# Turning six heads of a latent attention off TensorE, and dividing softmax rows on ScalarE

## The chip, the cores and the metric

The kernel runs on one core of a Trainium2 chip. The metric is device microseconds for one launch, lower is better. Before the change the median of three runs is 986.88 us (985.52 to 986.89). The profile shown here is of one execution that took 986.1 us, of which 984.3 us are the span from the first to the last recorded instruction.

## The reference: what is computed

A sequence of 256 tokens of width 1024 passes through two layers. Each layer is a half-step SwiGLU feed-forward block, a token mixer, a second half-step feed-forward block and a gated embedding; a last normalisation ends it. Layer 0 mixes with multi-head latent attention (chunk-causal, with a rotary part), layer 1 with forgetting attention (token-causal, with a decay bias). Both have 8 heads of width 128 and share this core:

```python
s = scores_fn(q0, q1)                        # (B, H, 128, q1), float32
s = jnp.where(allowed, s, NEG_INF)
probs = jax.nn.softmax(s, axis=-1).astype(v.dtype)
outs.append(jnp.einsum('bhqk,bkhd->bqhd', probs, v[:, :q1]))
```

The queries come in two blocks of 128; block 0 sees 128 keys, block 1 all 256. So one head has a score tile of 128 rows (queries) by 384 columns: 128 columns for block 0, then 256 for block 1.

## The kernel before, in words

Everything is float32. Weights come from memory as raw tiles of 128 x 1024; ScalarE rounds each to a high part (L97) and VectorE takes the rest as a low part (L101), so that the matrix products of high and low parts on TensorE keep float32 accuracy. `Weights` keeps four raw tiles and seven pairs; its transfers (L88) are issued on SyncE's queue, in the order in which the program calls it.

Every engine takes its own instructions strictly in program order. The order is written out by hand: there is no scheduler that moves an instruction past another. So an instruction that waits holds up whatever stands behind it on its engine or on its transfer queue.

`attention` (L487) is called by both mixers and is a software pipeline over steps h. In step h it does, in this order:

- `shares(h-2)`: VectorE takes the reciprocal of the softmax sums (L520) and multiplies the two parts of the row tile by it (L521, L522).
- `low()`: VectorE computes the low part of head outputs that are pending (L565, recorded at L228).
- `project(h, 0)`: the first half of what makes queries and keys of a later head. In the latent attention that is at most some products and their copies to SBUF (L707 to L721); in the forgetting attention it is a whole block of eight weight products.
- some "fills" (`fill_some`): products of finished heads with the output weights, put in to keep TensorE busy.
- the turn of a head, so that keys lie on the partitions, as the value product wants them.
- `scores(h-1)`: the score products on TensorE, then on VectorE the masked copy with its row maximum (L501) and the bias (L505 or L510/L511), then two exponentials with row sums on ScalarE (L513, L514).
- `project(h, 1)`, a weight tile's low part in some steps, more fills.
- `values`: the value products (L557, L558), and the copy of the result to SBUF by ScalarE (L559).

There are two ways to turn a head. `turn` (L539) uses TensorE: three 128 x 128 transposes (L543) into PSUM, then a copy to SBUF on ScalarE (L545). The other way is used for heads below `moved`: VectorE transposes the 32 x 32 blocks of the tile (L526), four transfers on SyncE's queue write it to memory so that whole rows come to lie right (L531), and `back` (L533) reads it in again with one transfer (L536).

The two mixers differ in their parameters. The latent attention (`mla`, L787) has `lag` 3, which the code calls `late`, and `moved` 0: every head is turned on TensorE in step h = head + 3 and its values follow in the same step. The forgetting attention (`fox`, L889) has `lag` 2 and `moved` 6: heads 0 to 5 go through memory and get their values one step after `back`, heads 6 and 7 are turned on TensorE. The fills per step are fixed tables: `MLA_FILLS` (L45) gives, for the latent attention, 3 fills in step 6, 4 in step 7, 1 + 5 in step 8, 4 + 3 in step 9 and 2 + 2 in step 10. `ready` (L620, L638) says for how many heads a fill may be made; a fill that is not possible yet is left for the loop behind the pipeline (L647). Four output blocks (`early`) are open for fills.

In the latent attention, step 1 also issues four transfers of rotary query parts on SyncE's queue (L720, L721), and step 3 four more.

## Time and profile before

| what | value |
|---|---|
| median of 3 runs | 986.88 us (985.52 to 986.89) |
| the profiled execution | 986.1 us, span 984.3 us |
| TensorE (PE) busy | 975.3 us |
| VectorE (DVE) busy | 735.5 us |
| ScalarE (ACT) busy | 507.4 us |
| GpSimd (POOL) busy | 428.2 us |
| steps of the latent attention | about 212 to 246 us of the span |
| steps of the forgetting attention | about 688 to 748 us of the span |

The profile has a page of totals and several views of the same trace. The timeline of an engine lists its instructions with start and duration in us; in brackets stands how long the engine had been idle before and who released it. Starts of neighbouring rows give the real pace, since instructions of one engine overlap at their ends. The view of one source line gives the shortest, middle and longest duration in ns of its instructions and, for a transfer, the time from its issue to its landing. PE is TensorE, SPq is the queue of transfers that SyncE issues.

### The profile page before, as it was taken

How to read it: one execution, taken by the hardware profiler on the slowest of the kernel's cores; microseconds unless marked ns; L12 is line 12 of the kernel's file. 1: busy time of each engine (PE TensorE's matmuls, PEld its weight loads, DVE VectorE, ACT ScalarE, POOL GpSimd, SP SyncE). 2: the span in 40 equal slices, each digit the busy share in tenths (PEclk: the TensorE clock that was granted, in tenths of full speed). 3: DMA queues.
4: the chain of work that ended last, by engine and by line, in shares of the span. 5: the costliest groups of instructions: out<-in, count | busy, mean ns of one | idle time of the engine just before them, and what ended most of it. 6: DMA issues, size and time to landing. Idle time of an engine off the chain costs nothing.

```text
span 984.3 us, 15934 instructions
## 1 busy us (share of the span) xinstructions
PE 975.3 (99%) x5766; PEld 861.4 (88%) x5766; DVE 735.5 (75%) x1097; ACT 507.4 (52%) x796; POOL 428.2 (44%) x374
## 2 busy tenths in 40 slices
PE   9999999999999999999999999999999999999997
PEld 7888888998988888889888888889889888888886
DVE  6777878686867787667887876666997677786585
ACT  7555544466545554545555544545445455544361
POOL 0777731110357775111477773122231377771010
PEclk9999999999999999999999999999999999999999
DMA  8677666564456666665367666557773566666581
GB/s 324 187 250 208 199 184 183 185 197 124 127 161 210 213 204 188 190 201 194 107 199 212 196 183 197 176 174 240 234 214 113 180 192 209 207 194 192 137 280 56
DMA packets 67166, 187.53 MB, mean 191 GB/s; under 512 B 18724, under 2 KB 21168, under 8 KB 66960
## 3 DMA queue, kind: packets, MB, share of 16 engines
q1 hardware_dynamic: 65904, 183.94, 61.2%
q0 software_dynamic: 608, 1.72, 0.5%
q8 instruction: 46, 0.75, 0.3%
q10 hardware_dynamic: 576, 0.85, 0.3%
q14 instruction: 32, 0.26, 0.1%
HBM read 181.88 MB, written 2.24 MB: 187 GB/s over the span
## 4 chain that ended last, share of the span: by engine, by line
PE 94%; DVE 2%; ACT 1%; issue 1%; DMA 1%; POOL 0%; SPq 0%; POOLq 0%; DVEq 0%; ACTq 0%
PE po L247 17%; PE pu L247 16%; PE pg L247 16%; PE po L248 8%; PE pg L248 8%; PE pu L248 8%; PE ps L247 5%; PE ps L248 2%; PE ps L234 2%; PE ps L232 2%; PE ps L233 2%; PE pv L232 1%; PE pv L234 1%; PE pv L233 1%; PE po L557 1%; DVE wlo L101 1%
## 5 line engine op out<-in xcount | busy, mean ns | idle before, releaser
L101 DVE TENSOR_TENSOR wlo<-raw,whi 128x1024 fp32r<-128x1024 f32 (+2 forms) x339 | 416.4, 1235 | 28.3 <-ACT whi L97 28.1
L97 ACT ACTIVATE whi<-raw 128x1024 fp32r<-128x1024 f32 (+2 forms) x339 | 336.0, 1023 | 40.6 <-DMA raw<-in_ffn_in_dram 14.7
L390 POOL TENSOR_TENSOR gu<-two 128x256 f32<-128x256 f32 x176 | 217.7, 1238 | 113.7 <-DVE two L388 107.1
L247 PE MATMUL pg<-u,whi 128*128 128x512 f32 x702 | 251.2, 395 | 0.0
L247 PE MATMUL pu<-u,whi 128*128 128x512 f32 x702 | 250.9, 395 | 0.0
L247 PE MATMUL po<-hs,whi 128*128 128x512 f32 x704 | 246.8, 394 | 0.0
L248 PE MATMUL pg<-u,wlo 128*128 128x256 f32 x702 | 197.3, 281 | 0.5 <-DVE wlo L228 0.3
L248 PE MATMUL po<-hs,wlo 128*128 128x256 f32 x704 | 197.3, 280 | 0.0
L248 PE MATMUL pu<-u,wlo 128*128 128x256 f32 x702 | 196.8, 280 | 0.0
L247 PEld LDWEIGHTS po<-hs,whi 128*128 128x128 f32 x704 | 132.1, 188 | 31.3
L247 PEld LDWEIGHTS pu<-u,whi 128*128 128x128 f32 x702 | 131.8, 188 | 31.0
L247 PEld LDWEIGHTS pg<-u,whi 128*128 128x128 f32 x702 | 131.8, 188 | 30.9 <-ACT whi L1099 0.2
L248 PEld LDWEIGHTS pg<-u,wlo 128*128 128x128 f32 x702 | 132.0, 188 | 2.0 <-DVE wlo L101 1.1
L248 PEld LDWEIGHTS po<-hs,wlo 128*128 128x128 f32 x704 | 132.3, 188 | 0.0
L248 PEld LDWEIGHTS pu<-u,wlo 128*128 128x128 f32 x702 | 132.0, 188 | 0.0
L408 POOL TENSOR_TENSOR hid<-sg,gu 128x256 f32<-128x256 f32 x88 | 121.1, 1376 | 6.9
L303 POOL TENSOR_TENSOR acc<-acc,sq 128x256 f32<-128x256 f32 x42 | 43.2, 1028 | 178.6 <-ACT sq L298 156.3
L224 ACT ACTIVATE hs<-hid 128x256 fp32r<-128x256 f32 x88 | 36.8, 418 | 155.7 <-POOL hid L408 155.7
L228 DVE TENSOR_TENSOR hs<-hid,hs 128x256 fp32r<-128x256 f32 x88 | 54.1, 615 | 71.3 <-ACT hs L224 71.3
L287 ACT ACTIVATE u<-state 128x256 fp32r<-128x256 f32 x47 | 24.0, 511 | 122.7 <-DVE state L467 102.4
L388 DVE TENSOR_TENSOR two<-pg,rb 128x512 f32<-128x512 f32 x88 | 60.0, 682 | 28.9 <-PE pg L248 19.4
L467 DVE SCALAR_TENSOR_TENSOR state<-po,state 128x256 f32<-128x256 f32 x64 | 27.1, 424 | 60.2 <-PE po L248 59.1
(258 smaller groups left out, 1157.6 us busy)
## 6 DMA issues: line engine op xcount, KB each, us to landing
raw<-in_ffn_in_dram SPq DMA_DIRECT2D x172, 512.0 KB, 4.2
raw<-in_ffn_out_dram SPq DMA_DIRECT2D x64, 512.0 KB, 4.2
raw<-in_ffn_out_dram SPq DMA_DIRECT2D x32, 384.0 KB, 3.4
raw<-in_fox_qk_dram SPq DMA_DIRECT2D x16, 512.0 KB, 4.4
raw<-in_mla_o_dram SPq DMA_DIRECT2D x8, 512.0 KB, 5.9
raw<-in_ple_gate_dram SPq DMA_DIRECT2D x8, 512.0 KB, 4.2
raw<-in_fox_o_dram SPq DMA_DIRECT2D x8, 512.0 KB, 3.9
raw<-in_ple_rows_dram SPq DMA_DIRECT2D x8, 512.0 KB, 4.8
```

The costliest lines, as they stand in the source:

```text
L97: self.nc.scalar.activation(self.pairs[i][0][:, c], self.raws[i][:, c], AF.Copy)
L101: self.nc.vector.tensor_sub(lo[:, c], self.raws[i][:, c], hi[:, c].bitcast(F32))
L224: nc.scalar.activation(hi, src, AF.Copy)
L228: nc.vector.tensor_sub(lo, src, hi.bitcast(F32))
L232: nc.tensor.matmul(ps, w[0], x[0], start=first, stop=False)
L233: nc.tensor.matmul(ps, w[1], x[0], start=False, stop=False)
L247: nc.tensor.matmul(ps, hi, x[:, k], start=k == 0, stop=False)
L248: nc.tensor.matmul(ps[:, 1, :], lo, x[:, k, 0, :], start=False, stop=k == last)
L303: nc.gpsimd.tensor_add(new, self.acc, sq)
L388: nc.vector.tensor_mul(two, ps, norm.rb2)
L390: nc.gpsimd.tensor_add(gu[c, i], two[:, 0, :], two[:, 1, :])
L408: nc.gpsimd.tensor_mul(hid[c], gu.pop((c, 0)), gu.pop((c, 1)))
```

## The change

In both attentions the two multiplications by the reciprocal go, for heads below `moved`, from VectorE to ScalarE (a copy with a scale for each partition). What followed them in `shares` becomes a function `out`, called after `low()`: the block transpose on VectorE, then one transfer that writes the tile as it lies. `back` now gathers: four transfers, each of 32 partitions with four pieces of 96 numbers. In the forgetting attention all four are on SyncE's queue; in the latent attention two of them are on GpSimd's queue.

The latent attention gets `moved` 6. Its heads 0 to 5 are no longer turned on TensorE; `back` for a head stands at the start of step head + 3, behind `out` of the next head, and its values stand at the end of step head + 4. Heads 6 and 7 are as they were. The first `ready` of a step is one lower while moved heads are under way. The blocks are kept in a part of the `kqv` tile that lies idle. `MLA_FILLS` does not change. Pending low parts are now done in the order in which they came.

```diff
--- before.py
+++ after.py
@@ -518,22 +518,28 @@
             pr, den = probs[h]
             inv = work.tile([P, 2], F32, name="inv", bufs=3)
             nc.vector.reciprocal(inv, den)
-            nc.vector.tensor_scalar(pr[:, :P], pr[:, :P], inv[:, 0:1], None, op0=ALU.mult)
-            nc.vector.tensor_scalar(pr[:, P:], pr[:, P:], inv[:, 1:2], None, op0=ALU.mult)
-            if h < moved:
-                pr, _ = probs.pop(h)
-                squares = room[h % 2]
-                nc.vector.transpose(squares.rearrange("p (k u c) -> p k u c", k=4, u=3),
-                                    pr.rearrange("p (u k c) -> p k u c", u=3, k=4))
-                turned[h] = dram.tile([P, 3 * P], F32, name="keys", bufs=2)
-                to = turned[h].rearrange("(k r) (q n) -> q r k n", k=4, q=4)
-                for q in range(4):
-                    nc.sync.dma_start(to[q], squares[q * 32:(q + 1) * 32, :].rearrange("r (k n) -> r k n", k=4))
+            for i, a in enumerate((slice(0, P), slice(P, 3 * P))):
+                if h < moved:
+                    nc.scalar.activation(pr[:, a], pr[:, a], AF.Copy, scale=inv[:, i:i + 1])
+                else:
+                    nc.vector.tensor_scalar(pr[:, a], pr[:, a], inv[:, i:i + 1], None, op0=ALU.mult)
+
+        def out(h):
+
+            pr, _ = probs.pop(h)
+            squares = room[h % 2]
+            nc.vector.transpose(squares.rearrange("p (k u c) -> p k u c", k=4, u=3),
+                                pr.rearrange("p (u k c) -> p k u c", u=3, k=4))
+            turned[h] = dram.tile([P, 3 * P], F32, name="keys", bufs=3)
+            nc.sync.dma_start(turned[h], squares)
 
         def back(h):
 
             p = work.tile([P, 3 * P], F32, name="ptS", bufs=3)
-            nc.sync.dma_start(p, turned[h])
+            src = turned[h].rearrange("(q r) (k n) -> k r q n", q=4, k=4)
+            for k in range(4):
+                (nc.gpsimd if late and k % 2 else nc.sync).dma_start(
+                    p[k * 32:(k + 1) * 32, :].rearrange("r (q n) -> r q n", q=4), src[k])
             turned[h] = p
 
@@ -562,7 +568,7 @@
             while lows:
-                rest(*lows.pop())
+                rest(*lows.pop(0))
@@ -613,15 +619,19 @@
             if 0 <= h - 2 < H:
                 shares(h - 2)
             low()
+            if 0 <= h - 2 < moved:
+                out(h - 2)
+            if late and 0 <= h - lag < moved:
+                back(h - lag)
             if h == H and not late:
                 W.pump()
             if late:
 
-                ready = h - lag - 1
+                ready = h - lag - 1 - (0 < h - lag <= moved)
             if h < H:
                 project(h, 0)
             fill_some(fills.get((h, 0), 0))
-            if 0 <= h - lag < moved:
+            if not late and 0 <= h - lag < moved:
                 back(h - lag)
             if moved <= h - lag:
                 turn(h - lag)
@@ -689,6 +699,7 @@
         kT, qT, qr = kq[:, :8, :], kq[:, 8:16, :], kq[:, 16:24, :]
+        squares = [kr[:, a:a + 2, :].rearrange("p s n -> p (s n)")[:, :3 * P] for a in (2, 4)]
@@ -784,7 +795,7 @@
-        attention(project, score, v, lambda h: (chunks[:, P:], chunks), qscale, nxt, 3, MLA_FILLS, 4)
+        attention(project, score, v, lambda h: (chunks[:, P:], chunks), qscale, nxt, 3, MLA_FILLS, 4, moved=H - 2, room=squares)
```

## The prediction

> **What bounds the kernel now.** I read the page first, then the waits, then the timelines of the engines in the latent attention, then the transfers.

> ```profile
> span 984.3 us, 15934 instructions
> PE 975.3 (99%) x5766; PEld 861.4 (88%) x5766; DVE 735.5 (75%) x1097; ACT 507.4 (52%) x796; POOL 428.2 (44%) x374
> ...
> PEclk9999999999999999999999999999999999999999
> ...
> PE 94%; DVE 2%; ACT 1%; issue 1%; DMA 1%; POOL 0%; SPq 0%; POOLq 0%; DVEq 0%; ACTq 0%
> ```

> ```profile
> PE cold L1090 <- DVE warm L1087: 1.1, 1, 1.1
> ```

> TensorE (PE) is busy 975.3 of 984.3 us, and 94% of the chain that ended last is its work. The longest wait of PE in the trace is 1.1 us, at the start. So any product removed is time gained, and any new wait of PE is time lost, wherever PE stands in its order. What has to be asked is whether the six heads' keys are in SBUF when PE comes to their values.

> The rows of PE in the latent attention, each with its start and duration:

> ```profile
> 218.81 0.49 PE L543 MATMUL pt<-ident,pr 128*128 128x128 f32 x3
> ...
> 222.24 0.49 PE L543 MATMUL pt<-ident,pr 128*128 128x128 f32 x3
> 222.57 0.82 PE L782 MATMUL psc<-kqv 128*128 128x128 f32 x4
> ...
> 224.58 0.61 PE L557 MATMUL po<-ptS,kqv 128*128 128x256 f32 x2
> ...
> 225.25 0.49 PE L543 MATMUL pt<-ident,pr 128*128 128x128 f32 x3
> ...
> 231.07 0.59 PE L557 MATMUL po<-ptS,kqv 128*128 128x256 f32 x2
> ...
> 232.05 0.82 PE L782 MATMUL psc<-kqv 128*128 128x128 f32 x4
> ...
> 234.77 0.60 PE L557 MATMUL po<-ptS,kqv 128*128 128x256 f32 x2
> ...
> 245.77 0.48 PE L247 MATMUL ps<-os,whi 128*128 128x512 f32 x1
> ...
> 246.54 0.39 PE L247 MATMUL ps<-os,whi 128*128 128x512 f32 x1
> ...
> 246.89 0.40 PE L247 MATMUL ps<-os,whi 128*128 128x512 f32 x1
> ```

> By starts: a turn costs PE 0.33 us (222.24 to 222.57), not the 0.49 of its row; scores with the six or three products behind them 2.01 (222.57 to 224.58); values 0.67 (to 225.25), 0.65 where fills follow; a fill 0.35 (246.54 to 246.89); scores with four fills 2.72 (232.05 to 234.77), so scores alone 1.32 and with three fills 2.37. The values of head 3 start at 231.07; those of head 7 are over at 245.77.

> VectorE and ScalarE hand each head to and fro, and that loop has a time of its own:

> ```profile
> 218.06 0.16 DVE L520 RECIPROCAL inv<-den 128x2 f32<-128x2 f32 x1
> ...
> 226.96 0.17 DVE L520 RECIPROCAL inv<-den 128x2 f32<-128x2 f32 x1 [0.64 <-ACT pr L514]
> ...
> 227.62 0.42 DVE L228 TENSOR_TENSOR os<-po,os 128x256 fp32r<-128x256 f32 x1
> 227.96 0.28 DVE L501 CUSTOM_DVE_ANT_0 pr<-psc,chunks 128x128 f32<-128x128 f32 x1
> ...
> 228.62 0.16 DVE L505 SCALAR_TENSOR_TENSOR nm<-m,qscale 128x2 f32<-128x2 f32 x1
> ...
> 230.08 0.17 DVE L520 RECIPROCAL inv<-den 128x2 f32<-128x2 f32 x1 [0.64 <-ACT pr L514]
> ```

> ```profile
> 228.88 0.49 ACT L513 ACTIVATE pr<-pr,nm,qscale 128x128 f32<-128x128 f32 x1 [1.31 <-DVE nm L505]
> 229.28 0.19 ACT L513 ACTIVATION_READ_ACCUMULATOR pr<-pr,nm,qscale 128x1 f32 x1
> 229.37 0.58 ACT L514 ACTIVATE pr<-pr,nm,qscale 128x256 f32<-128x256 f32 x1
> ```

> From reciprocal (226.96) to reciprocal (230.08) it is 3.12 us: 0.66 for reciprocal and divisions, 0.34 for the low part of an older head, 0.66 for the masked copies, then 0.26 to the first exponential, and 1.20 for both until the next reciprocal, for which VectorE has waited 0.64. PE's own step there is 3.01 (222.24 to 225.25). Both are close; a longer loop is not hidden for long.

> **The change, part by part.**

> *Turns removed.* Six of the eight turns of the latent attention go from PE: 6 x 0.33 = 1.98 us. This is all that PE can gain, and nothing else of PE's work changes but order. The strided read of the value product costs nothing extra: forgetting attention reads so already, at the same pace (row 708.38 below). The six copies out of PSUM on ScalarE go too; they were in nobody's way.

> *Divisions on ScalarE, and the transpose in the loop.* VectorE's next masked copy now stands behind the transpose, that behind ScalarE's two divisions, and those behind the reciprocal. The nearest row for a division is a copy with a scale per partition; for the transpose it is the forgetting attention's:

> ```profile
> L287 ACT ACTIVATE u<-state 128x256 fp32r<-128x256 f32 x47 | 24.0, 511 | 122.7 <-DVE state L467 102.4
> ```

> ```profile
> 698.25 0.16 DVE L520 RECIPROCAL inv<-den 128x2 f32<-128x2 f32 x1
> ...
> 699.03 0.58 DVE L526 STREAM_TRANSPOSE kqv<-pr 128x384 f32<-128x384 f32 x1
> 699.54 0.65 DVE L872 TENSOR_TENSOR two<-ps,rb 128x512 f32<-128x512 f32 x1
> ...
> 722.40 0.69 DVE L872 TENSOR_TENSOR two<-ps,rb 128x512 f32<-128x512 f32 x1 [0.20 <-PE ps L248]
> ```

> The division of 128 x 256 takes 0.51, that of 128 x 128 0.09 less (as the two exponentials differ), and the second starts 0.09 before the first ends (228.88 + 0.49 against 229.28): 0.84 for both. With 0.17 for the reciprocal and hand-overs of 0.10 and 0.04 (the bias ends at 228.78, its exponential starts at 228.88), the transpose starts 1.15 us after the reciprocal, and the masked copy 0.51 later. The older head's low part now falls into the wait for ScalarE. New loop: 1.15 + 0.51 + 2.12 (227.96 to 230.08) = 3.78 us against 3.12, in six steps. Bounds: 3.6 if ScalarE takes 0.66 like VectorE now, 3.9 if its pair does not overlap.

> So reciprocals, which start in step 2 at 218.06, come 3.78 apart, as 221.84, 225.62, 229.40, 233.18 and 236.96 for heads 1 to 5, and each transpose ends 1.73 after its own: heads 0 to 4 at 219.79, 223.57, 227.35, 231.13 and 234.91.

> *The way through memory.* The rows of the forgetting attention, of GpSimd's queue, and of SyncE's queue in the steps in question:

> ```profile
> L531 SPq DMA_DIRECT2D keys<-kqv x24: 318/426/678, 699.6 to 734.5; - x24
> ...
> DMA to landing us min/median/max: 2.0/2.7/3.4
> ```

> ```profile
> L536 SPq DMA_DIRECT2D ptS<-keys x6: 337/338/338, 703.5 to 736.7; - x6
> ...
> DMA to landing us min/median/max: 2.7/3.1/4.0
> ```

> ```profile
> L352 POOL DMA_DIRECT2D rb<-row x3: 577/577/582, 274.4 to 776.5; - x3
> ...
> DMA to landing us min/median/max: 3.3/4.4/5.0
> ```

> ```profile
> 220.03 1.32 SPq L88 DMA_DIRECT2D raw<-in_mla_o_dram  x2
> ...
> 703.49 0.34 SPq L536 DMA_DIRECT2D ptS<-keys  x1
> ```

> No row shows a write of a whole tile or a gather in four; I bound the write by 2.0 to 3.4 and take 2.7, a piece on SyncE's queue by 2.7 to 4.0 and take 2.9, one on GpSimd's by 3.3 to 5.0 and take 4.4, the medians of the nearest rows (the pieces are smaller than the reading row's). An issue costs 0.43 on SyncE, 0.58 on GpSimd, which does nothing else in these steps. `back` of a head stands behind `out` of the next one on SyncE's queue, so its pieces there wait for the next head's transpose: that is the wait the change adds, and behind it stand four rotary transfers and weight tiles, whose users come later.

> Now PE's order. Step 3 starts at 218.81. Without turn and values, two times 2.01 brings PE to the values of head 0 at 222.83. Their keys: the first of the two weight tiles goes out on SyncE at 220.03 and I put the write behind it, at 220.6; it lands at 223.3 or, as loads of 512 KB are under way, up to 225.0; the next head's write is issued at 223.6, and the pieces on SyncE follow from 224.1 to 224.5 and land at about 227.4; those on GpSimd land from 223.3 + 0.58 + 4.4 = 228.3 on. I take 228.3: **PE waits 5.5 us.** Then the later heads:

> - Head 1: PE comes at 228.3 + 0.65 + 2.01 = 230.96. Keys: transpose of head 2 ends at 227.35, + 0.05 + 0.40 + 0.43 + 2.9 = 231.1, GpSimd's 223.6 + 2.7 + 0.58 + 4.4 = 231.3. Values at 231.3.
> - Head 2: PE at 231.3 + 0.65 + 2.37 = 234.3; keys at 231.13 + 3.8 = 234.9. Values at 234.9.
> - Head 3: PE at 234.9 + 0.65 + 2.72 = 238.3; keys at 234.91 + 3.8 = 238.7, GpSimd's at 231.17 + 2.7 + 0.58 + 4.4 = 238.85. Values at 238.7.
> - Head 4 and on: PE has 0.65 + 0.35 + 1.32 + 5 x 0.35 = 4.07 us of work first and comes at 242.8, keys at 242.5: no more waits.

> From there to the end of head 7's values it took 245.77 - 231.07 = 14.70 before. Of that fall away two turns (0.66), the scores of head 6 (1.32) and four fills (1.40), which now lie ahead; one fill of step 9 finds `ready` too low and is made behind the pipeline instead, the same 0.35 of work. So the same work is done at 238.7 + 11.3 = 250.0 against 245.8: **+4.2 us**. That is 1.98 gained and about 6.2 more of waiting. Bounds: with 2.0 for writes and 2.7 for all pieces, head 0 at 227.1 and the chain by PE alone gives head 3 at 236.1, +1.7; with 3.4, 4.0 and 5.0 head 3 is at 240.2, +5.7. Behind this PE is the bound again and nothing is given back.

> [...]

> *The forgetting attention.* PE does the same. On VectorE, reciprocal to the next product goes from 1.29 (698.25 to 699.54, no older head pending) to 1.15 + 0.51 = 1.66; with a low part of 0.3 pending, which the new order hides, it is about even. VectorE waits 0.20 for PE in such steps (722.40), so two steps of + 0.37 are made up. ScalarE has room:

> ```profile
> 722.29 0.40 ACT L513 ACTIVATE pr<-pr,nm 128x128 f32<-128x128 f32 x1 [3.63 <-DVE nm L511]
> ```

> ```profile
> 708.38 0.59 PE L557 MATMUL po<-ptS,kqv 128*128 128x256 f32 x2
> ```

> Head 0's keys landed near 703.49 + 3.1 = 706.6 and were wanted at 708.38. Transpose 0.4 later, three issues fewer and three more of 0.43: about 0.4 later in all, covered by 1.8. I take 0, with - 0.2 and + 0.8 as ends (nothing that PE waits for goes away; VectorE's 0.74 wholly passed on).

> *The rest* (order of pending low parts, a third buffer for keys) costs nothing: PE has fills between.

> Sum: 986.1 + 4.2 = 990.3 against the profiled execution. The median of the runs is 0.8 above that execution; I put half of it on top: **990.7**.

> **The rivals.**

> *The waits stay hidden* (faster). Two steps between transpose and values cover the way through memory, and only the 1.98 of the turns is left: 986.1 - 2.0 + 0.4 = 984.5. It decides at 2.0 us of PE's waits in all. For it: a step more was given. Against it: 222.83 minus 219.79 leaves 3.0 us for a write and a read that take 2.7 and 3.1 one after the other.

> *One wait, then PE sets the pace.* The loop stays near 3.3, or the transfers land early; PE waits once for head 0 and then follows its own work: + 1.7 to + 2.9, say 989.2.

> *The clock falls.* PE has no wait of over 1.1 us now and its granted clock stands at nine tenths or more in all 40 slices. If 5.5 us of idleness halved its rate until it waits again, 2.66 us of work between heads 0 and 1 become 5.3, head 1 comes at 233.6, head 2 at 236.6, head 3 at 240.0: + 5.5, 992.0. [...] Slow transfers (+ 5.7) end in the same place.

> **How the numbers follow.** Forecast 0.50, one wait 0.20, clock or slow transfers 0.15, waits hidden 0.07, an end within 2 us of before 0.08. 0.2% (2.0 us) is about what a measurement can tell. Slower: the forecast, the clock and most of "one wait", 0.82; the same 0.11; faster 0.07. The range takes the forecast, one wait and the clock, and their bounds: 987.8 to 993.2.

> **What would show it right or wrong.** In the changed profile: no rows of L543 before step 9 of the latent attention; PE idle some 4 to 6 us ahead of the first L557 there, released by a transfer of `ptS`; shorter idles ahead of the next three; reciprocals 3.7 to 3.9 us apart in steps 2 to 7; a wait of VectorE for ScalarE of 0.3 to 0.8 us ahead of each transpose; PE in the forgetting attention without waits. It is wrong if the first L557 waits under 2 us, if reciprocals stay near 3.1 apart, or if PE waits in the forgetting attention.

## The result, and the profile after

| | median | lowest to highest | profiled execution | its span |
|---|---|---|---|---|
| before | 986.82 us | 985.52 to 990.31 | 986.1 us | 984.3 us |
| after | 996.42 us | 994.99 to 998.59 | 994.99 us | 993.2 us |

The ratio is 1.0099, with a 95% interval of 1.0086 to 1.0113: 9.6 us slower, where the forecast was 3.9 and the range ended at 993.2. The sign was right and the size too small.

The page of the changed kernel: span and busy time, the granted clock in 40 slices, the chain that ended last.

```profile
span 993.2 us, 15932 instructions
PE 976.2 (98%) x5748; PEld 860.9 (87%) x5748; DVE 731.8 (74%) x1079; ACT 514.1 (52%) x814; POOL 434.8 (44%) x386
...
PEclk9999999998999999999999999999999999999999
...
PE 86%; DVE 5%; DMA 3%; ACT 2%; issue 2%; SPq 1%; POOL 1%; POOLq 0%; ACTq 0%; DVEq 0%
```

PE has 18 products fewer and is yet busy 0.9 us longer: some of its work has become slower. One digit of the clock's row, the tenth, is an 8. That slice is 223 to 248 us, in the latent attention. The chain now runs for 3% over transfers (1% before).

The waits of PE, in all, times, longest:

```profile
PE po L563 <- DMA ptS<-keys: 5.5, 1, 5.5
PE po L563 <- issue: 1.5, 1, 1.5
...
PE pst L317 <- POOL acc L303: 1.0, 1, 1.0
PE ps L247 <- DVE os L228: 0.3, 1, 0.3
```

L563 is the value product, L557 before. The wait for GpSimd (L303) lies at 960.23, in the last norm: e1 below has it too (0.91), e9, the changed kernel again, has not. From PE's timeline the first rows of heads 0, 1 and 5, the scores behind heads 0 and 1, and the product that follows head 7's values:

```profile
228.19 1.19 PE L563 MATMUL po<-ptS,kqv 128*128 128x256 f32 x2 [5.54 <-DMA ptS<-keys]
229.60 1.49 PE L793 MATMUL psc<-kqv 128*128 128x128 f32 x4
...
233.00 0.59 PE L563 MATMUL po<-ptS,kqv 128*128 128x256 f32 x2
233.66 0.82 PE L793 MATMUL psc<-kqv 128*128 128x128 f32 x4
...
249.25 0.67 PE L563 MATMUL po<-ptS,kqv 128*128 128x256 f32 x2 [1.46 <-issue]
...
253.28 0.48 PE L247 MATMUL ps<-os,whi 128*128 128x512 f32 x1
```

PE waits 5.54 us for head 0 and 1.46 for head 5. Heads 1 to 4 wait for nothing. The values of head 7 are over at 253.28, where the forecast had 250.0. Right behind the first wait scores take 1.49 us, a head later 0.82. The table by stretches of 2 us gives the reason; its columns are busy time of PE, of the weight loads, of VectorE, ScalarE and GpSimd, then the granted clock, the share of the DMA engines and GB/s:

```profile
224.00:226.00 2.00, 0.00 (x0) 0.00 (x0) 0.64 (x3) 1.65 (x6) 0.95 (x2) 0.91 0.85 311
226.00:228.00 2.00, 0.00 (x0) 0.00 (x0) 1.85 (x7) 0.74 (x3) 0.88 (x3) 0.50 0.64 174
228.00:230.00 2.00, 1.81 (x6) 1.67 (x7) 0.17 (x1) 0.59 (x3) 0.42 (x1) 0.50 0.64 153
230.00:232.00 2.00, 2.00 (x9) 1.73 (x7) 1.00 (x2) 0.91 (x3) 0.90 (x2) 0.50 0.39 114
232.00:234.00 2.00, 2.00 (x11) 1.72 (x11) 1.52 (x6) 0.72 (x3) 0.18 (x1) 0.88 0.63 176
```

The clock falls to 0.50 inside the wait and comes back at about 232.5 (0.88 is 0.5 for the first 0.48 us). PE works from 228.19 to then at half rate: 4.3 us in which 2.1 us of work are lost.

**Where the time lies.** I measure one stage: from the last norm ahead of the latent attention to the first product of the output blocks that no fill touches. The two rows of PE's timeline before, and the two after:

```profile
197.16 0.50 PE L317 MATMUL pst<-ones,acc 128*128 128x1 f32 x4
...
251.45 0.28 PE L232 MATMUL ps<-os,whi 128*128 128x256 f32 x1
```

```profile
196.81 0.50 PE L317 MATMUL pst<-ones,acc 128*128 128x1 f32 x4
...
259.35 0.28 PE L232 MATMUL ps<-os,whi 128*128 128x256 f32 x1
```

54.29 us have become 62.54: + 8.25 of the 8.9 us between the two spans. Three waits (5.54 + 1.46 + 0.29 = 7.29), less 1.98 for the turns, make + 5.31; the half rate + 2.1. The other 0.8 stand in no bracket, but the starts of neighbouring rows show them. Ends of rows overlap, so by starts each of the three waits is 0.16 longer (5.70, 1.62 and 0.46): + 0.5. Three shorter hold-ups (ahead of 242.78, 244.48 and 251.07) cost 0.4, slower first products behind them 0.3, and the 0.4 that PE lost in this way before the change is gone. The forecast of waits was 6.2 in this stage, of the clock nothing.

### The profile page after: what moved, and what is told of

It is laid out like the page before. It is cut to its first block, busy times and chain, and to the rows that moved or that the text cites. A ratio compares the mean times of both kernels' runs of the same rounds, so it can differ in the third digit from the quotient of the medians.

```text
span 993.2 us, 15932 instructions
## 1 busy us (share of the span) xinstructions
PE 976.2 (98%) x5748; PEld 860.9 (87%) x5748; DVE 731.8 (74%) x1079; ACT 514.1 (52%) x814; POOL 434.8 (44%) x386
## 4 chain that ended last, share of the span: by engine, by line
PE 86%; DVE 5%; DMA 3%; ACT 2%; issue 2%; SPq 1%; POOL 1%; POOLq 0%; ACTq 0%; DVEq 0%
PE pu L247 15%; PE pg L247 15%; PE po L247 14%; PE pg L248 8%; PE pu L248 8%; PE po L248 7%; PE ps L247 5%; PE ps L248 2%; DVE wlo L101 2%; PE ps L234 1%; PE ps L232 1%; PE ps L233 1%; SPq L926 1%; PE pv L232 1%; PE po L563 1%
## 5 line engine op out<-in xcount | busy, mean ns | idle before, releaser
L97 ACT ACTIVATE whi<-raw 128x1024 fp32r<-128x1024 f32 (+2 forms) x339 | 335.6, 1022 | 40.9 <-DMA raw<-in_ffn_in_dram 11.3
L247 PE MATMUL pg<-u,whi 128*128 128x512 f32 x702 | 251.1, 395 | 0.0
L247 PE MATMUL pu<-u,whi 128*128 128x512 f32 x702 | 250.9, 395 | 0.0
L247 PE MATMUL po<-hs,whi 128*128 128x512 f32 x704 | 246.8, 394 | 0.0
L248 PE MATMUL pg<-u,wlo 128*128 128x256 f32 x702 | 197.3, 281 | 0.5 <-DVE wlo L101 0.2
L248 PE MATMUL po<-hs,wlo 128*128 128x256 f32 x704 | 197.2, 280 | 0.0
L248 PE MATMUL pu<-u,wlo 128*128 128x256 f32 x702 | 196.8, 280 | 0.0
L247 PEld LDWEIGHTS po<-hs,whi 128*128 128x128 f32 x704 | 132.1, 188 | 31.3
L247 PEld LDWEIGHTS pu<-u,whi 128*128 128x128 f32 x702 | 131.8, 188 | 31.0
L247 PEld LDWEIGHTS pg<-u,whi 128*128 128x128 f32 x702 | 131.8, 188 | 30.9
L248 PEld LDWEIGHTS pg<-u,wlo 128*128 128x128 f32 x702 | 132.0, 188 | 1.9 <-DVE wlo L101 0.9
L248 PEld LDWEIGHTS po<-hs,wlo 128*128 128x128 f32 x704 | 132.3, 188 | 0.0
L248 PEld LDWEIGHTS pu<-u,wlo 128*128 128x128 f32 x702 | 132.0, 188 | 0.0
L303 POOL TENSOR_TENSOR acc<-acc,sq 128x256 f32<-128x256 f32 x42 | 43.3, 1031 | 179.5 <-ACT sq L298 157.7
L228 DVE TENSOR_TENSOR hs<-hid,hs 128x256 fp32r<-128x256 f32 x88 | 53.6, 609 | 72.4 <-ACT hs L224 72.4
L287 ACT ACTIVATE u<-state 128x256 fp32r<-128x256 f32 x47 | 24.0, 511 | 123.1 <-DVE state L467 102.5
L467 DVE SCALAR_TENSOR_TENSOR state<-po,state 128x256 f32<-128x256 f32 x64 | 27.1, 424 | 60.1 <-PE po L248 59.0
```

The source lines that it names most:

```text
L97: self.nc.scalar.activation(self.pairs[i][0][:, c], self.raws[i][:, c], AF.Copy)
L228: nc.vector.tensor_sub(lo, src, hi.bitcast(F32))
L247: nc.tensor.matmul(ps, hi, x[:, k], start=k == 0, stop=False)
L248: nc.tensor.matmul(ps[:, 1, :], lo, x[:, k, 0, :], start=False, stop=k == last)
L287: nc.scalar.activation(self.pair[:, b, 0, c], src[:, c], AF.Copy, scale=g)
L303: nc.gpsimd.tensor_add(new, self.acc, sq)
```

## The experiments

Theory when they began: PE's one long wait lowers the clock, and the clock, not the waits, is what the forecast lacks. Rivals: the VectorE–ScalarE loop has become the bound; or the forms chosen (ScalarE's divisions, gathers in four) are the price. All times are medians, ratios against the kernel before on the same chip; "stage" is the stage above in the profiled execution, against 54.29.

| run | median us | ratio, 95% interval | stage |
|---|---|---|---|
| e1_fox_only | 987.21 | 1.0005 (0.9995 to 1.0015) | + 0.04 |
| e2_mla_only | 996.66 | 1.0092 (1.0077 to 1.0107) | + 8.96 |
| e3_no_wait | 992.42 | 1.0049 (1.0036 to 1.0062) | + 5.07 |
| e4_warm | 991.86 | 1.0043 (1.0030 to 1.0056) | + 6.14 |
| e5_late_out | 995.40 | 1.0081 (1.0059 to 1.0102) | + 6.97 |
| e6_late_out_warm | 992.97 | 1.0054 (1.0030 to 1.0078) | + 7.27 |
| e7_vector_divides | 995.52 | 1.0086 (1.0061 to 1.0110) | + 8.36 |
| e8_old_route | 995.44 | 1.0082 (1.0058 to 1.0105) | + 10.41 |
| e9_after_again | 994.95 | 1.0085 (1.0071 to 1.0098) | + 7.79 |
| e10_warm_again | 991.96 | 1.0055 (1.0042 to 1.0068) | + 6.31 |
| e11_warm_half | 993.12 | 1.0065 (1.0053 to 1.0077) | + 7.04 |
| e12_no_wait_late_out | 989.58 | 1.0023 (1.0010 to 1.0037) | + 2.44 |
| e13_two_steps_more | 997.63 | 1.0112 (1.0096 to 1.0129) | + 11.33 |
| e14_two_steps_more_late_out | 995.53 | 1.0085 (1.0070 to 1.0100) | + 8.91 |
| e15_no_wait_late_out_warm | 988.53 | 1.0023 (1.0012 to 1.0033) | + 2.32 |

Outside the stage the spans of single executions differ by some 3 us (929.2 to 932.2 in these runs, 930.0 before), so differences of one us between a stage and a median mean nothing.

### Which attention: e1_fox_only, e2_mla_only

e1 leaves the latent attention as it was:

```diff
-        attention(project, score, v, lambda h: (chunks[:, P:], chunks), qscale, nxt, 3, MLA_FILLS, 4, moved=H - 2, room=squares)
+        attention(project, score, v, lambda h: (chunks[:, P:], chunks), qscale, nxt, 3, MLA_FILLS, 4)
```

> The forgetting attention has the new form (ScalarE divides, whole tile written, gathered in four), the latent attention is as before. Theory (the latent attention alone pays): 986.8, at most 1 above the kernel before, no wait of TensorE in the forgetting attention. Rival (divisions on ScalarE and the gather cost in both attentions): 2 us or more above before.

e2 leaves the forgetting attention as it was:

```diff
-                if h < moved:
+                if late and h < moved:
                     nc.scalar.activation(pr[:, a], pr[:, a], AF.Copy, scale=inv[:, i:i + 1])
...
-            nc.sync.dma_start(turned[h], squares)
+            if not late:
+                to = turned[h].rearrange("(k r) (q n) -> q r k n", k=4, q=4)
+                for q in range(4):
+                    nc.sync.dma_start(to[q], squares[q * 32:(q + 1) * 32, :].rearrange("r (k n) -> r k n", k=4))
+            else:
+                nc.sync.dma_start(turned[h], squares)
...
+            if not late:
+                nc.sync.dma_start(p, turned[h])
+                turned[h] = p
+                return
```

> The latent attention has the new form, the forgetting attention is as before. Theory: 995.5 to 996.5, nearly all of the changed kernel's loss. Rival (the forgetting attention pays a share): 994 or less.

The forgetting attention's new form costs + 0.35 us with an interval across zero; the latent attention's has the whole loss.

### The clock: e4_warm, e9_after_again, e10_warm_again, e11_warm_half

e4 gives PE 46 products of zeros, whose result nobody reads, ahead of head 0's values. e9 is the changed kernel and e10 is e4, both again on one chip; e11 has 23 products.

```diff
+            if late and h == lag + 1:
+                idle = bank("cold", (P, T))
+                for _ in range(46):
+                    nc.tensor.matmul(idle, warm[:, :P], warm, start=True, stop=True)
             if 0 <= h - lag - 1 < moved:
                 values(h - lag - 1)
```

> The changed kernel with 46 products of zeros (bfloat16, result unused) ahead of the first value products of the latent attention, about 5 us of work where TensorE waits 5.5. Theory (the fall of the clock is one part of the miss, the head loop held by TensorE another): granted clock stays at 1.0 in the stage, 994 to 995.5. Rival (the fall of the clock is all of the miss against the forecast): 992 or less. Second rival (the clock costs nothing, it falls while TensorE would wait anyway): 996.

> The changed kernel itself, on the same chip as the next two. 996 to 997; a first wait of 5 to 6 us, granted clock 0.5 for about 6 us after its first half.

> The changed kernel with 46 products of zeros ahead of the first values, again. Theory (the fall of the clock is the larger part of what the forecast missed): 4 to 5 us under the changed kernel, 991.5 to 992.5. Rival (the difference between the two earlier runs was the chips' or the runs'): 994 or more.

> The same with 23 products, about 2.6 us of work, so that TensorE is idle for about 3 us instead of 5.5. Theory (a wait has to be longer than some 3 us for the clock to fall): granted clock 1.0 in the stage and the time of the run with 46. Rival (the clock falls after any wait of a few us): granted clock 0.5 behind the wait and 994 or more.

e4 came to the rival's value (992 or less), not to the 994 to 995.5 of the theory. It is 4.8 us faster than e2 on the same chip (which differs otherwise in the forgetting attention alone); e10 is 3.0 faster than e9, less than the 4 to 5 expected. e9 itself, put at 996 to 997, came to 994.95. PE's timeline in e10:

```profile
223.03 5.20 PE L653 MATMUL cold<-warm 128*128 128x256 bf16 x46
...
229.97 0.67 PE L563 MATMUL po<-ptS,kqv 128*128 128x256 f32 x2 [1.75 <-DMA ptS<-keys]
233.22 0.67 PE L563 MATMUL po<-ptS,kqv 128*128 128x256 f32 x2 [0.34 <-DVE m L501]
247.85 0.67 PE L563 MATMUL po<-ptS,kqv 128*128 128x256 f32 x2 [0.23 <-issue]
```

and one row of its table by stretches:

```profile
230.00:232.00 2.00, 2.00 (x13) 1.86 (x13) 0.42 (x1) 1.07 (x3) 0.00 (x0) 1.00 0.73 221
```

The values of head 0 take 0.67, not 1.19, and the stretch in which the changed kernel made 9 products at half rate holds 13. From their start to PE's arrival at head 5's (the start there less its wait) the same work takes 247.62 - 229.97 = 17.65 us, 0.34 of it waiting; in the changed kernel 247.79 - 228.19 = 19.60, in e9 247.35 - 228.37 = 18.98. So with the clock held the same work is 1.3 to 2.0 us shorter. The medians of e9 and e10 are further apart (3.0) than the stages of their two profiled executions (1.5); that difference stays open. In e10 head 0's keys came 1.2 later in the stage, and head 5's wait was 1.2 shorter, since its write landed sooner: the products remove nothing of head 0's wait.

What is left is near the forecast: 5.20 + 1.75 + 0.34 + 0.23 - 1.98 = 5.5 by rows, + 5.2 by medians (e4: + 5.0); its stage shows + 6.3, so the 0.8 that no bracket shows is there too.

With 23 products neither theory nor rival of e11 held: PE was idle for 4.2 us behind them (225.6 to 229.81), the clock fell, but only after PE had gone on, and the time (993.12) lies between the two:

```profile
228.00:230.00 2.00, 0.19 (x1) 0.22 (x2) 0.49 (x2) 0.86 (x4) 1.09 (x2) 1.00 0.44 107
230.00:232.00 2.00, 2.00 (x8) 1.79 (x8) 0.42 (x1) 0.95 (x3) 0.29 (x1) 0.56 0.73 194
```

### Without the wait for keys: e3_no_wait

The value products of heads 0 to 5 in the latent attention read a tile that has long been in SBUF, so these heads' outputs are not computed from their own rows; everything else is still done.

```diff
-    def attention(project, score, v, mask, scale, nxt, lag, fills, early, cumq=None, moved=0, room=None):
+    def attention(project, score, v, mask, scale, nxt, lag, fills, early, cumq=None, moved=0, room=None, stand=None):
...
+            if late and h < moved:
+                p = stand
             if h < moved:
                 p = p.rearrange("p (q u c) -> p u q c", q=4, u=3)
...
-        attention(project, score, v, lambda h: (chunks[:, P:], chunks), qscale, nxt, 3, MLA_FILLS, 4, moved=H - 2, room=squares)
+        attention(project, score, v, lambda h: (chunks[:, P:], chunks), qscale, nxt, 3, MLA_FILLS, 4, moved=H - 2, room=squares,
+                  stand=kq[:, 0:2, :].rearrange("p s n -> p (s n)")[:, :3 * P])
```

> The changed kernel, but the value products of heads 0 to 5 of the latent attention read a tile that has been in SBUF for long; blocks, transfers and divisions are still made. So TensorE waits for no transfer; the output of these heads is not the attention's. Theory (TensorE's waits for transfers and what follows from them are the whole loss): 985 to 988, reciprocals still about 3.6 us apart. Rival (the longer loop of VectorE and ScalarE is the loss): 991 or more.

I had expected 985 to 988: all waits gone and the turns gained. It came to 992.42, the rival's value, so the theory that keys alone hold PE fell. PE's waits in the latent attention:

```profile
PE ps L247 <- DVE os L228: 4.9, 2, 3.0
```

PE now waits for low parts of head outputs (L228), which the fills need. They stand in VectorE's loop, whose reciprocals still come 3.6 us apart, while PE's steps without turns are shorter (2.7 us, from the values at 223.05 to those at 225.71); and the clock fell again, to 0.50 in 232 to 236 and for some time on both sides. The loop is a second limit, hidden behind the first.

### The order in VectorE's loop: e5_late_out, e6_late_out_warm, e12_no_wait_late_out, e15_no_wait_late_out_warm

In e5 transpose and write come behind the next head's masked copies, so that these do not wait for ScalarE's divisions:

```diff
-            if 0 <= h - 2 < moved:
+            if not late and 0 <= h - 2 < moved:
                 out(h - 2)
...
                 scores(h - 1)
+            if late and 0 <= h - 2 < moved:
+                out(h - 2)
```

e6 adds e4's 46 products to this, and e12 adds e3's tile (heads 0 to 5 from other data, as there). e15 is e12 with 22 products of zeros ahead of the fills of step 6:

```diff
+            if late and h == 6:
+                idle = bank("cold", (P, T))
+                for _ in range(22):
+                    nc.tensor.matmul(idle, warm[:, :P], warm, start=True, stop=True)
             fill_some(fills.get((h, 1), 0))
```

> The changed kernel, but in the latent attention the block transpose and its write stand behind the masked copies of the next head instead of ahead of them (so back of the head before is issued ahead of them, too). Theory (the transpose in the VectorE-ScalarE loop is one of two limits, the first wait for transfers the other): reciprocals 2.7 to 3.0 us apart where TensorE does not hold them, first wait of TensorE still 5 to 6 us with the clock falling, 994 to 995.5. Rival (the loop is no limit as long as the transfers are): 996 to 997. Second rival (the loop is the limit): 990 or less.

> The same with the 46 products of zeros ahead of the first values: loop short, clock held. What is left is the wait for transfers itself. Theory: 5.5 us of first wait less 2 us of turns, 989 to 990.5. Rival (waits of later heads remain whatever the loop does): 991.5 or more.

> Value products of heads 0 to 5 of the latent attention read a tile long in SBUF (their output is not the attention's), and block transpose and write stand behind the masked copies. So both limits are taken away, the wait for transfers and the transpose in the loop. Theory (these two, and the clock behind their waits, are the whole loss): reciprocals 2.7 us apart, no wait of TensorE over 2 us, clock 1.0, 985 to 987.5. Rival (something else in the new form costs, for instance the added traffic or GpSimd's queue): 989 or more.

> Value products of heads 0 to 5 read a tile long in SBUF (output not the attention's), transposes behind the masked copies, and 22 products of zeros ahead of the fills of step 6, where TensorE waited 2.85 us for a low part and the clock fell. Theory: clock 1.0, 986.5 to 988. Rival (not the clock but something else made that run 2.8 us slower than before): 989 or more.

In e5 the first reciprocals do come closer (3.6, 2.1 and 2.5 us apart), but head 0's keys are no earlier (PE waits 5.72), and then VectorE itself stands still:

```profile
231.04 0.43 DVE L228 TENSOR_TENSOR os<-po,os 128x256 fp32r<-128x256 f32 x1 [4.39 <-ACT os L565]
```

It waits for ScalarE's copy of head 0's values (L565), which PE makes late, and the next reciprocal comes 8.8 us after the one before. So a late head 0 also holds the engines that feed the later heads: PE, ScalarE and VectorE form one ring, through their orders. In e6 heads 0 to 3 wait 0.81, 1.14, 0.50 and 1.20 at a clock of 1.00; it is no better than e4 and came to the rival's value (991.5 or more).

In e12 one wait is left, and it takes the clock with it:

```profile
231.00 0.80 PE L247 MATMUL ps<-os,whi 128*128 128x512 f32 x1 [2.85 <-DVE os L228]
```

```profile
230.00:232.00 2.00, 1.00 (x3) 0.90 (x4) 1.66 (x8) 1.34 (x3) 0.62 (x2) 0.75 0.57 144
232.00:234.00 2.00, 2.00 (x9) 1.73 (x8) 0.61 (x2) 1.50 (x6) 0.42 (x1) 0.50 0.37 119
234.00:236.00 2.00, 2.00 (x12) 1.81 (x12) 1.91 (x6) 1.17 (x4) 0.67 (x2) 0.90 0.65 197
```

2.85 - 1.98 + 1.7 for 3.4 us at half rate (1.0 + 2.0 + 0.4) = 2.6; measured + 2.44. At 989.58 it reaches its rival's 989, but the traffic or GpSimd's queue that the rival named is not what the trace shows. VectorE's transposes wait, 1.18, 1.12 and 1.70 us, for a write to land:

```profile
233.39 0.58 DVE L531 STREAM_TRANSPOSE kqv<-pr 128x384 f32<-128x384 f32 x1 [1.70 <-DMA keys<-kqv]
```

The transpose of a head goes into one of two blocks in turn (`room[h % 2]`), and the write of two heads before has to be out of it. So here two blocks are a limit of their own; a third was not tried. In e15 the clock stays at 1.00, and the waits (1.7) and products (2.57) less 1.98 are 2.3; measured + 2.32. It is just above the 986.5 to 988 that I gave it. With keys that cost PE nothing, the loop and its writes, through two blocks, still make it wait longer (2.85 in e12) than the turns are worth (1.98).

### The forms: e7_vector_divides, e8_old_route

e7 divides on VectorE again in the latent attention. e8 has there the four writes and one reading transfer of the forgetting attention before, all on SyncE's queue (e2's branches, with `late` for `not late`).

```diff
-                if h < moved:
+                if h < moved and not late:
                     nc.scalar.activation(pr[:, a], pr[:, a], AF.Copy, scale=inv[:, i:i + 1])
```

> The changed kernel, but in the latent attention VectorE divides, as before. By the rows the loop is then 0.66 + 0.50 + 0.34 + 2.12 = 3.6 us, the same as measured with ScalarE. Theory (the engine that divides does not matter, the transpose in the loop does): within 1.5 us of the changed kernel. Rival (handing the division to ScalarE is a cost of its own): 993 or less.

> The changed kernel, but in the latent attention the tile is written in four pieces and read back whole, all on SyncE's queue, as the forgetting attention did before. Theory (the length of the way through memory counts, not its form): first wait of TensorE 5 to 6 us, within 1.5 us of the changed kernel. Rival (the whole write, which landed after 4.8 us, or GpSimd's queue is at fault): 993.5 or less.

Neither differs in its median from the changed kernel by more than the intervals. In e7 reciprocals are 3.3 to 3.4 us apart until head 0's wait, and the first wait is still 5.10. In e8 it is 6.7, above the 5 to 6 expected, and PE waits once more, after which the clock falls a second time:

```profile
243.18 0.77 PE L572 MATMUL po<-ptS,kqv 128*128 128x256 f32 x2 [1.62 <-DMA ptS<-keys]
```

```profile
242.00:244.00 2.00, 0.82 (x4) 0.74 (x5) 1.69 (x4) 1.05 (x4) 0.00 (x0) 0.91 1.00 292
244.00:246.00 2.00, 2.00 (x8) 1.81 (x8) 0.42 (x1) 1.33 (x2) 0.00 (x0) 0.50 1.08 282
```

That is part of its long stage (+ 10.41). Its profiled execution, 996.73 us, is also the longest of its runs. By the medians, dividing engine and form of the transfers are not the price.

### More time for the transfers: e13_two_steps_more, e14_two_steps_more_late_out

All values of the latent attention come two steps later, with two tiles more for keys; e14 adds e5's order.

```diff
-        for h in range(H + lag):
+        for h in range(H + lag + hold):
...
-            if 0 <= h - lag - 1 < moved:
-                values(h - lag - 1)
-            if moved <= h - lag:
-                values(h - lag)
+            if 0 <= h - lag - hold - 1 < moved:
+                values(h - lag - hold - 1)
+            if moved <= h - lag - hold:
+                values(h - lag - hold)
...
-        attention(project, score, v, lambda h: (chunks[:, P:], chunks), qscale, nxt, 3, MLA_FILLS, 4, moved=H - 2, room=squares)
+        attention(project, score, v, lambda h: (chunks[:, P:], chunks), qscale, nxt, 3, MLA_FILLS, 4, moved=H - 2, room=squares, hold=2)
```

(Fills, `ready` and the turns of heads 6 and 7 move by `hold` as well.)

> The changed kernel, but in the latent attention values (and the turns of heads 6 and 7, and the table of fills) come two steps later still, with five buffers for keys read back; back stays where it is. Theory (two limits: the first wait, and the loop with the transpose in it): the first wait falls to 1 to 2 us and the clock stays at 1.0, but heads come 3.6 us apart and head 5's keys are in SBUF only at about 245, so 990 to 991.5. Rival (distance was all that was missing): 985.5 or less.

> The same, and block transpose and write stand behind the masked copies. Theory: heads about 2.7 us apart, head 5's keys at about 242, no wait over 2 us, 986.5 to 988: the loss goes, and little of the 2 us of turns is kept. Rival (the way through memory costs by itself, wherever it is put): 990 or more.

Neither did what was expected: e13 (997.63) lies above theory (990 to 991.5) and rival alike, e14 (995.53) at its rival's value. In e13:

```profile
228.40 0.94 PE L563 MATMUL po<-ptS,kqv 128*128 128x256 f32 x2 [2.38 <-DMA ptS<-keys]
...
236.43 0.51 PE L247 MATMUL ps<-os,whi 128*128 128x512 f32 x1 [2.21 <-DVE os L228]
240.41 0.79 PE L247 MATMUL ps<-os,whi 128*128 128x512 f32 x1 [3.35 <-DVE os L228]
```

Two steps more gave only 3.2 us (5.54 to 2.38), since a step of PE without values or turns is 2.0 us long (220.53 to 222.53) while the loop needs 3.6 for a head: PE runs into the loop. The clock fell twice, at 228 to 232 and at 239 to 246. In e14 two waits of 1.99 and 1.43 for keys left the clock alone; one of 3.09 for a low part then lowered it.

## Why the prediction was right or wrong

**Head 0's wait** was forecast at 5.5 us and is 5.54. Its parts were not as forecast. The chain that ended last shows them in the changed kernel:

```profile
219.96 4.81 DMA keys<-kqv
224.76 0.28 issue
225.05 0.60 POOL ptS L541
225.65 2.34 DMA ptS<-keys
228.19 1.19 PE po L563 x2
```

The write was issued 0.6 earlier than I put it and took 4.81 instead of 2.7; GpSimd's second piece took 2.34 instead of 4.4. Two wrong sizes cancelled, so the match of the total is luck. For the write I had bounds of 2.0 to 3.4 from four smaller transfers, and it lies outside them. Landing times of the write and of the pieces in both attentions, and the pieces by queue in the latent one (KB each, median):

```profile
L534 SPq DMA_DIRECT2D keys<-kqv x12: 326/338/523, 220.0 to 741.3; - x12
...
DMA to landing us min/median/max: 1.9/4.0/4.8
```

```profile
ptS<-keys SPq DMA_DIRECT2D x12, 48.0 KB, 2.3
ptS<-keys POOLq DMA_DIRECT2D x12, 48.0 KB, 2.5
```

For GpSimd's pieces I took the 4.4 us of a row of 128 KB; pieces of 48 KB took 2.5, so that row was no measure for them.

**The loop** was forecast at 3.78 us and VectorE's wait ahead of a transpose at 0.3 to 0.8. VectorE's timeline after:

```profile
222.34 0.58 DVE L531 STREAM_TRANSPOSE kqv<-pr 128x384 f32<-128x384 f32 x1 [0.87 <-ACT pr L523]
...
224.88 0.17 DVE L520 RECIPROCAL inv<-den 128x2 f32<-128x2 f32 x1 [0.50 <-ACT pr L514]
...
228.46 0.17 DVE L520 RECIPROCAL inv<-den 128x2 f32<-128x2 f32 x1 [0.58 <-ACT pr L514]
230.26 0.42 DVE L228 TENSOR_TENSOR os<-po,os 128x256 fp32r<-128x256 f32 x1 [1.63 <-ACT os L565]
...
232.40 0.29 DVE L501 CUSTOM_DVE_ANT_0 pr<-psc,chunks 128x128 f32<-128x128 f32 x1 [0.88 <-PE psc L795]
...
234.48 0.17 DVE L520 RECIPROCAL inv<-den 128x2 f32<-128x2 f32 x1 [0.52 <-ACT pr L514]
```

It is 3.6 where nothing disturbs it, the lower bound of the forecast, and the wait ahead of the first three transposes is 0.87 or 0.86. Then comes 6.02 (228.46 to 234.48): 1.63 us of waiting for head 0's late values and 0.88 for PE's scores at half rate. My loop was an interval of VectorE and ScalarE alone, and head 0's wait was not fed back into it.

**Later heads.** The waits that the forecast lists add up to 6.8 us (5.5 + 0.3 + 0.6 + 0.4), not to its 6.2, which is net: most of the 0.6 between is a hold-up of PE before, ahead of the values at 221.49 (0.33 by starts), that goes with the turns, and values counted at 0.65 that took up to 0.76. Heads 1 to 3 were to wait 1.3 us together; they did not, neither at half rate nor, but for 0.34, with the clock held. "Head 4 and on: no more waits" failed: head 5 waited 1.46. Its write went out at 239.70 and the reads at 244.00, 4.3 us later; in e10 it was 3.3, and the wait 0.23. Why that write varies was not tried.

**The clock: the step that failed.** The forecast kept it full across a wait of 5.5 us. It was a rival, with a chance of 0.15 and + 5.5 us: it had 2.66 us of work at half rate, 2.7 us lost, of which shorter waits of later heads took back half. Half rate came for 4.3 us of PE's work and cost 2.1, somewhat less, but heads 1 to 4 had no waits that could take any of it back. That rival's half rate, until PE waits again, was an assumption: the kernel before has no wait of over 1.1 us and so does not show it. The changed kernel shows 0.50, but back at 1.00 (232.47) while PE was at work, after 4.3 us at half rate (3.1 in e9); and waits of 2.38 (e13) and, in e8, even of 1.62 came with a fall. For an assumption that bore on the longest wait of the sum, 0.15 was too little.

**Together:** waits of 7.3 came where the forecast had a net 6.2, 1.1 more; 2.1 from the clock; 0.8 that no bracket shows: 4.2 + 4.0 = 8.2 against 8.25 in the stage. The clock is the largest missing term, but not the only one: 990.7 + 2.1 alone would be 992.8, just inside the range. With the clock held the result is 991.9 to 992.0 (e4, e10), inside the range. Between stage (+ 8.25) and medians (+ 9.6) 1.3 us stay open; executions differ by that much elsewhere, and the same kernel in e9 is 8.2 above before by its median.

**Right:** the sign; the price of the turns (by starts, those in the stage take 2.47 us before and 0.49 after); that the forgetting attention costs nothing that can be measured (e1). In the changed kernel's trace PE waits for no transfer there; in e9's it does once, for about 0.3 us.

No version tried beats the kernel before, and by e12 the loop with its writes, as built, takes back what the turns give.

## What to carry to other kernels

Before you take work off the engine that sets the pace, follow one item round the whole ring (values, copy, division, transpose, write, read, values) in the order of every engine: the slowest loop bounds the gain (here 3.6 us a head), and a first wait is passed on to it. If your own sum holds a wait of TensorE as long as those around which the clock fell here (2.38 us and longer, once 1.62), price the clock with it, at some 1.5 to 2.6 us of lost work (e9, e14) and with a chance of its own: between 1.6 and 2.0 us it fell here once (e8) and mostly not. When two sizes in a sum are taken from unlike rows, a matching total says nothing on either.
